# Norm sums and spreads as matrix products, a convolution finish through PSUM, and low weight parts queued behind the taps

## The chip, the cores and the metric

The kernel runs on one core of one Trainium2 chip. The metric is device time in microseconds of one execution. Before the change the median of three runs is 1796.49 us, and they lie between 1795.98 and 1796.54 us.

## What is computed

Two layers over a sequence of 512 tokens with 1024 features, all in float32. Each layer is

```
x = x + 1/2 * SwiGLU_1(RMSNorm(x))                       # 1024 -> 2816 -> 1024
h = RMSNorm(x);  [conv_a | conv_g | q | k | v] = h @ W_in  # five times 512 columns
  conv group: u = a * sigmoid(g); causal depthwise conv, 31 taps; RMSNorm over 512 channels; silu
  diff group: 4 heads, q and k normed per head of 64, two softmax maps with a bias by distance,
              A1 - lambda * A2, times v (128 wide), RMSNorm per head
x = x + concat(conv_out, diff_out) @ W_out
x = x + 1/2 * SwiGLU_2(RMSNorm(x))
```

## The kernel before

**Layout.** Features lie on the 128 partitions and tokens along the free dimension: `x` is eight tiles of 128x512. Every large product is made of three float32r products (`mm3`, L161 to L167): an operand is cut into a high part (rounded to float32r) and a low part (the rest), and high x high, high x low and low x high are summed in PSUM. `parts_of` (L96) makes the parts of a weight chunk: ScalarE copies the high part, and VectorE, or GpSimd where `eng` says so, subtracts to get the low part (L101). `chunk` (L103) loads a chunk through SyncE's DMA queue (SP) and calls it. The rings of weight buffers are five raw, four high and four low.

**The norms.** ScalarE squares each tile of `x`, and GpSimd adds the squares into one tile `s`. `rows_rstd` (L217) transposes the four 128x128 blocks of `s` on TensorE into the PSUM bank "y", VectorE sums each row (L225), scales and adds epsilon (L226), and GpSimd raises to the power -1/2 (L214). This gives a column of 1/rms per token, tokens on partitions. `spread` (L229) brings it back along the free dimension: VectorE multiplies the identity by the column (a diagonal, L241), TensorE multiplies a matrix of ones by that (L245) into bank "y", and ScalarE copies the bank to SBUF (L249). With `split` the column is first cut in two parts, and two float32r products are made. The six norms over 1024 features are in the four feed-forward blocks (split spread) and at the two mixers' inputs (unsplit). The products with the normed input run before the norm is known; its factor is put in when the banks are evicted (L458, L460, L568, L574).

**The feed-forward blocks** use a seven-product scheme on halves (`Halves`, `seven`) for 17 of their 22 column tiles. The change touches only the norm at their start (`first_products` L302, or the lambdas in `ffn` at L450 and L451).

**The mixer** (L541) first makes the convolution's inputs and q, k and v. Then come attention in 16 steps (four query blocks, the last block of tokens first, by four heads) and the convolution's taps:
- A step's scores (`softmaxes`, L714) go into one bank "sc" and one bank "po", two of each. VectorE adds the bias and finds the minimum (L718), ScalarE takes the exp (L722), and VectorE joins the two maps (L725, L727, L728). Two steps later TensorE transposes the map (L735), ScalarE copies it (L737), and a step later TensorE multiplies it by the values (L744).
- After a block's fourth head the per-head norm follows: `se` (L751) and `so` (L755, L756), a power on GpSimd (L214), the multiply `ov` (L759), transposes (L771), and the parts for the out projection (L773, L774).
- `conv_taps`: of the four channel tiles, tile 0 has its 31 taps, and tile 3 ten of its taps, as ScalarE products (L667) summed by GpSimd (L668). VectorE does the others (L680) in bank "y", and joins tile 3's two sums at L684. `conv_square` squares each tile on ScalarE (L654) and adds the squares on GpSimd (L655).
- `conv_finish` (L689) comes after the attention steps in the program's text. It takes the norm of the convolution, then per tile: a GpSimd multiply (L694), a tanh on ScalarE (L696), (tanh + 1) times the value on VectorE (L697), and the high and low parts (L698 on ScalarE, L699 on VectorE).
- The out projection (L815) takes the four convolution tiles first, for all 512 tokens (`ps_out`, 96 products of 512 columns), then the four attention tiles in two halves of the tokens. Its low weight parts are made by GpSimd.

**What sets the order.** The text is not the order. The Tile framework schedules the instructions of each engine by a timeline of its own when the kernel is built, and each engine then runs its queue strictly in that order. `tc.keep_in_program_order` holds single instructions in the text's order. Semaphores and the rings of tiles and banks set the waits.

## Time and profile before

| | us |
|---|---|
| median of 3 runs | 1796.49 |
| the profiled execution | 1796.31 |
| its span on the core | 1794.5 |
| TensorE busy, share of the span | 1784.6 (99%) |
| VectorE busy | 1211.1 (67%) |
| ScalarE busy | 896.1 (50%) |
| GpSimd busy | 653.6 (36%) |

The span is the time between the first and the last instruction of the profiled execution; the execution's own time is 1.8 us longer. PE is TensorE, PEld its weight loads, DVE VectorE, ACT ScalarE, POOL GpSimd and SP SyncE. Products on TensorE overlap, so the duration of one in a group is not what it occupies; the distance between the starts of two is. The granted clock was 1.00 throughout. The names L... in what follows are lines of the kernel before; where a line exists only in the new kernel, the diff shows it.

### The profile page before, as it was taken

What the parts mean: (1) busy time and instruction counts of PE and PEld (TensorE: products, weight loads), DVE (VectorE), ACT (ScalarE), POOL (GpSimd) and SP (SyncE); (2) the same over time, 40 slices, a digit from 0 to 9 for tenths busy, and PEclk for the clock granted to TensorE, in tenths of its full rate; (3) what the DMA queues carried; (4) which work ended last, traced back from release to release, by engine and by line L of the source; (5) the groups of instructions that cost most, each with busy time, mean ns of one, the idle gap of its engine ahead of it and who ended that gap; (6) DMA issues with size and microseconds to landing.
All of it is one profiled execution on the core that took longest, in us unless ns stands there. A gap on an engine that the chain in (4) does not pass through costs nothing.

```text
span 1794.5 us, 28356 instructions
## 1 busy us (share of the span) xinstructions
PE 1784.6 (99%) x10845; PEld 1590.1 (89%) x10845; DVE 1211.1 (67%) x1863; ACT 896.1 (50%) x1482; POOL 653.6 (36%) x460
## 2 busy tenths in 40 slices
PE   9999999999999999999999999999999999999999
PEld 7899899888788899899888998998887888998997
DVE  6976477568867867477576765765788587673762
ACT  6555265445744456256433643654558354552651
POOL 4242232269843132133102312412797331322420
PEclk9999999999999999999999999999999999999999
DMA  7466476323212366466333654663231133664651
GB/s 243 107 179 183 108 181 176 118 94 94 71 48 83 94 165 188 106 171 189 105 94 98 171 167 120 177 179 118 71 114 51 48 106 91 166 178 112 180 150 59
DMA packets 111721, 231.24 MB, mean 129 GB/s; under 512 B 12151, under 2 KB 33414, under 8 KB 111584
## 3 DMA queue, kind: packets, MB, share of 16 engines
q1 hardware_dynamic: 91488, 191.93, 33.4%
q0 software_dynamic: 19808, 37.33, 12.5%
q8 instruction: 85, 1.39, 0.3%
q14 instruction: 52, 0.43, 0.1%
q10 hardware_dynamic: 288, 0.16, 0.0%
HBM read 227.26 MB, written 3.42 MB: 129 GB/s over the span
## 4 chain that ended last, share of the span: by engine, by line
PE 96%; DVE 2%; issue 1%; ACT 1%; DMA 0%; SPq 0%; ACTq 0%; DVEq 0%
PE ps_pair L384 38%; PE ps_d L166 9%; PE ps_d L163 9%; PE ps_d L167 9%; PE ps_pair L167 5%; PE ps_pair L166 5%; PE ps_pair L163 5%; PE ps_pair L596 2%; PE ps_pair L597 2%; PE ps_pair L598 2%; PE ps_out L163 1%; PE ps_out L166 1%; PE ps_sc L714 1%; PE ps_out L167 1%; DVE actl L263 1%; PE ps_v L628 1%
## 5 line engine op out<-in xcount | busy, mean ns | idle before, releaser
L100 ACT ACTIVATE whi<-wraw 128x1024 fp32r<-128x1024 f32 (+2 forms) x599 | 465.9, 802 | 609.5 <-PE ps_pair L384 225.7
L101 DVE TENSOR_TENSOR wlo<-wraw,whi 128x512 fp32r<-128x512 f32 (+2 forms) x556 | 526.0, 968 | 212.6 <-ACT whi L100 208.4
L384 PE MATMUL ps_pair<-acth,wlo 128*128 128x256 f32 x1088 | 308.5, 284 | 0.0
L384 PE MATMUL ps_pair<-actl,whi 128*128 128x256 f32 x1088 | 308.5, 284 | 0.0
L384 PE MATMUL ps_pair<-acth,whi 128*128 128x256 f32 x1088 | 308.4, 283 | 0.0
L166 PE MATMUL ps_d<-hl,whi 128*128 128x512 f32 x704 | 274.2, 390 | 0.0
L167 PE MATMUL ps_d<-hh,wlo 128*128 128x512 f32 x704 | 273.4, 390 | 0.0
L163 PE MATMUL ps_d<-hh,whi 128*128 128x512 f32 x704 | 268.7, 390 | 0.0
L384 PE MATMUL ps_pair<-th,wlo 128*128 128x256 f32 x816 | 231.3, 283 | 0.0
L384 PE MATMUL ps_pair<-tl,whi 128*128 128x256 f32 x816 | 231.2, 283 | 0.0
L384 PE MATMUL ps_pair<-th,whi 128*128 128x256 f32 x816 | 231.2, 283 | 0.0
L146 POOL TENSOR_TENSOR wraw<-wraw 128x512 f32<-128x512 f32 x68 | 101.8, 1497 | 339.5 <-DMA wraw<-in_gu 272.2
L141 POOL DMA_DIRECT2D wraw<-in_gu x68 | 82.0, 1207 | 392.4 <-DMA wraw<-in_gu 228.6
L384 PEld LDWEIGHTS ps_pair<-acth,whi 128*128 128x128 f32 x1088 | 209.1, 192 | 0.3
L384 PEld LDWEIGHTS ps_pair<-actl,whi 128*128 128x128 f32 x1088 | 209.0, 192 | 0.3
L384 PEld LDWEIGHTS ps_pair<-acth,wlo 128*128 128x128 f32 x1088 | 209.1, 192 | 0.0
L480 DVE SCALAR_TENSOR_TENSOR x<-ps_d,x 128x512 f32<-128x512 f32 x96 | 64.7, 689 | 179.6 <-PE ps_d L167 179.3
L166 PE MATMUL ps_pair<-actl,whi 128*128 128x512 f32 x448 | 175.0, 391 | 0.3
L163 PE MATMUL ps_pair<-acth,whi 128*128 128x512 f32 x448 | 174.4, 394 | 0.5 <-ACT whi L100 0.3
L167 PE MATMUL ps_pair<-acth,wlo 128*128 128x512 f32 x448 | 174.5, 391 | 0.0
L384 PEld LDWEIGHTS ps_pair<-tl,whi 128*128 128x128 f32 x816 | 156.7, 192 | 0.7
L384 PEld LDWEIGHTS ps_pair<-th,whi 128*128 128x128 f32 x816 | 156.7, 192 | 0.6
(176 smaller groups left out, 3268.9 us busy)
## 6 DMA issues: line engine op xcount, KB each, us to landing
wraw<-in_gu SPq DMA_DIRECT2D x208, 256.0 KB, 4.0
wraw<-in_gu SPq DMA_DIRECT2D x104, 512.0 KB, 3.7
wraw<-in_gu POOLq DMA_DIRECT2D x68, 512.0 KB, 5.7
wraw<-in_wqkv SPq DMA_DIRECT2D x24, 512.0 KB, 3.7
wraw<-in_dn SPq DMA_DIRECT2D x84, 128.0 KB, 3.1
wraw<-in_dn SPq DMA_DIRECT2D x32, 256.0 KB, 3.1
wraw<-in_wag SPq DMA_DIRECT2D x16, 512.0 KB, 3.6
wraw<-in_wout SPq DMA_DIRECT2D x16, 512.0 KB, 3.6
```

Of the source, the lines that this page charges most:

```text
L100: S.activation(hi, raw, AF.Copy)
L101: (eng or V).tensor_tensor(out=lo, in0=raw, in1=f32(hi), op=ALU.subtract)
L141: nc.gpsimd.dma_start(two.rearrange("p (b c) -> p b c", b=2), u[:, h[0]].unsqueeze(1).broadcast_to([P, 2, 512]), accum_op=ALU.add)
L146: G.tensor_tensor(more[:, h[0]], two[:, h[1]], whole[:, h[0]], op=ALU.add)
L163: first = T.matmul(ps, wh, xh, start=start, stop=False)
L166: T.matmul(ps, wh, xl, start=False, stop=False)
L167: T.matmul(ps, wl, xh, start=False, stop=stop)
L384: mm = T.matmul(ps, l, r, start=first and i == j == 0, stop=False, skip_group_check=True)
L480: V.scalar_tensor_tensor(x[:, m, :], ps, 0.5, x[:, m, :], op0=ALU.mult, op1=ALU.add)
L596: T.matmul(ps[n], xh[:, t], wh, start=k == 0, stop=False)
L597: T.matmul(ps[n], xh[:, t], wl, start=False, stop=False)
L598: T.matmul(ps[n], xl[:, t], wh, start=False, stop=k == KT - 1)
```

## The change

- `rows_rstd` takes a list of sum tiles. For each of the four blocks of 128 tokens it multiplies the block by one column of ones, and sums over the tiles of the list in PSUM. The transposes and the VectorE reduce are gone; the scale by 1/dim and epsilon reads PSUM.
- `spread_bank` replaces the diagonal: four float32 products with the column broadcast over 128 columns as weights and the identity as the moving operand. The split into two parts is gone everywhere.
- The last convolution square is no longer added by GpSimd; it goes into the list as a second tile.
- `conv_finish` stands at attention step 9 in the text, and takes the norm from a call placed right after the taps. VectorE multiplies the value, the gain and the spread, which it reads in its bank; tanh is written to bank "y" and read there by VectorE; the low part is a GpSimd subtraction.
- `se` is a ScalarE square.
- The four weight chunks of the out projection's first half are requested right behind the taps, and their low parts are held in the text's order there (`pin`).

```diff
@@ -93,17 +93,19 @@
         dt = F32 if "raw" in tag else F32R
         return wp.tile([P, n], dt, tag=tag, name=tag, bufs=RING[tag])
-    def parts_of(raw, hi, lo, eng=None, first=False):
+    def parts_of(raw, hi, lo, eng=None, first=False, pin=False):
         if first:
             V.tensor_scalar(hi, raw, 1.0, None, op0=ALU.mult)
         else:
             S.activation(hi, raw, AF.Copy)
-        (eng or V).tensor_tensor(out=lo, in0=raw, in1=f32(hi), op=ALU.subtract)
-    def chunk(src, eng=None):
+        low = (eng or V).tensor_tensor(out=lo, in0=raw, in1=f32(hi), op=ALU.subtract)
+        if pin:
+            tc.keep_in_program_order(low)
+    def chunk(src, eng=None, pin=False):
         raw, hi, lo = ring("wraw"), ring("whi"), ring("wlo")
         nc.sync.dma_start(raw, src)
-        parts_of(raw, hi, lo, eng)
+        parts_of(raw, hi, lo, eng, pin=pin)
         return hi, lo
     def gather(src, blocks, eng=None):
@@ -214,39 +216,33 @@
         G.tensor_tensor(y, v, mhalf[:, :n], op=ALU.pow)
         return y
-    def rows_rstd(s, dim, use="", pin=False):
-        ps = bank("y", "ps_rows")
+    def rows_rstd(sums, dim, use="", pin=False):
+        ps = bank("y", "ps_rows")[:, :NT]
         for j in range(NT):
-            mm = T.transpose(ps[:, j * P : (j + 1) * P], s[:, j * P : (j + 1) * P], ident)
+            for n, s in enumerate(sums):
+                mm = T.matmul(ps[:, j : j + 1], s[:, j * P : (j + 1) * P], ones[:, :1],
+                              start=n == 0, stop=n == len(sums) - 1)
+                if pin:
+                    tc.keep_in_program_order(mm)
+        v = small.tile([P, NT], F32, tag=f"rowv{use}", name="rowv")
+        V.tensor_scalar(v, ps, 1.0 / dim, EPS, op0=ALU.mult, op1=ALU.add)
+        return rsqrt(v, NT, use), v
+    def spread_bank(rc, pin=False):
+        ps = bank("y", "ps_spread")
+        for j in range(NT):
+            mm = T.matmul(ps[:, j * P : (j + 1) * P], rc[:, j : j + 1].broadcast_to([P, P]), ident, start=True, stop=True)
             if pin:
                 tc.keep_in_program_order(mm)
-        v = small.tile([P, NT], F32, tag=f"rowv{use}", name="rowv")
-        V.tensor_reduce(v, ps.rearrange("p (j c) -> p j c", j=NT), axis=AX.X, op=ALU.add)
-        V.tensor_scalar(v, v, 1.0 / dim, EPS, op0=ALU.mult, op1=ALU.add)
-        return rsqrt(v, NT, use), v
-    def spread(rc, tag, pin=False, split=False):
-        parts, dt, left = [rc], F32, ones
-        if split:
-            hi = small.tile([P, NT], F32R, tag="rc_hi", name="rc_hi")
-            V.tensor_scalar(hi, rc, 1.0, None, op0=ALU.mult)
-            lo = small.tile([P, NT], F32, tag="rc_lo", name="rc_lo")
-            V.tensor_tensor(lo, rc, f32(hi), op=ALU.subtract)
-            parts, dt, left = [f32(hi), lo], F32R, ones_r
-        ps = bank("y", "ps_spread")
-        for n, part in enumerate(parts):
-            dg = tmp.tile([P, NT, P], dt, tag=("diag", "sq")[n], name="diag", bufs=1 + n)
-            V.tensor_tensor(
-                dg, ident.unsqueeze(1).broadcast_to([P, NT, P]),
-                part.unsqueeze(2).broadcast_to([P, NT, P]), op=ALU.mult,
-            )
-            mm = T.matmul(ps, left, dg.rearrange("p j c -> p (j c)"), start=n == 0, stop=n == len(parts) - 1)
-            if pin:
-                tc.keep_in_program_order(mm)
+        return ps
+    def spread(rc, tag, pin=False):
         r = act.tile([P, SEQ], F32, tag=tag, name=tag)
-        S.activation(r, ps, AF.Copy)
+        S.activation(r, spread_bank(rc, pin), AF.Copy)
         return r
     class Prep:
@@ -303,11 +299,11 @@
         if not early:
-            rc, v = rows_rstd(pr.s, DM)
-            r = spread(rc, "rb", split=True)
+            rc, v = rows_rstd([pr.s], DM)
+            r = spread(rc, "rb")
         for k in range(KT):
             if early and k == STATS_AT:
-                rc, v = rows_rstd(pr.s, DM, pin=True)
+                rc, v = rows_rstd([pr.s], DM, pin=True)
             for i in range(2):
                 mm3(ps[0][i], wpart(w[0][i], k), pr[k], k == 0, k == KT - 1, pin=early and k in (0, STATS_AT))
         for i in range(2):
@@ -447,8 +443,8 @@
                     if m == 1:
                         _, _, r = first_products(pr, [h[1] for h in held], [h[2] for h in held])
                     elif r is None:
-                        rc = products(pr, w, held[-1][2][0], 0, 4, lambda: rows_rstd(pr.s, DM, pin=True)[0])
-                        r = products(pr, w, held[-1][2][1], 1, 3, lambda: spread(rc, "rb", pin=True, split=True))
+                        rc = products(pr, w, held[-1][2][0], 0, 4, lambda: rows_rstd([pr.s], DM, pin=True)[0])
+                        r = products(pr, w, held[-1][2][1], 1, 3, lambda: spread(rc, "rb", pin=True))
                     else:
                         for i in range(2):
                             products(pr, w, held[-1][2][i], i)
@@ -645,6 +641,7 @@
             ys = [None] * CT
             csum = mp.tile([P, SEQ], F32, tag="csum", name="csum")
+            csums = [csum]
             def conv_square(c, y):
                 if c == 0:
@@ -652,7 +649,10 @@
                 else:
                     sq = mt.tile([P, SEQ], F32, tag="csq", name="csq", bufs=1)
                     S.activation(sq, y, AF.Square)
-                    G.tensor_tensor(csum, csum, sq, op=ALU.add)
+                    if c == CT - 1:
+                        csums.append(sq)
+                    else:
+                        G.tensor_tensor(csum, csum, sq, op=ALU.add)
             def conv_taps(c, n):
@@ -686,17 +686,18 @@
                     S.activation(ys[c], y, AF.Copy)
                 conv_square(c, ys[c])
-            def conv_finish():
-                rcv = spread(rows_rstd(csum, CC, "c")[0], "rb")
+            def conv_finish(rc):
+                rcv = spread_bank(rc)
+                for c in range(CT):
+                    V.scalar_tensor_tensor(ys[c], ys[c], ghalf[l][:, c : c + 1], rcv, op0=ALU.mult, op1=ALU.mult)
                 for c in range(CT):
                     z = ys[c]
-                    hg = ghalf[l][:, c : c + 1]
-                    G.tensor_tensor(z, z, rcv, op=ALU.mult)
-                    th = mt.tile([P, SEQ], F32, tag="gl", name="th", bufs=1)
-                    S.activation(th, z, AF.Tanh, scale=hg)
+                    th = bank("y", "ps_th")
+                    S.activation(th, z, AF.Tanh)
                     V.scalar_tensor_tensor(z, th, 1.0, z, op0=ALU.add, op1=ALU.mult)
-                    S.activation(ch[:, c, :], z, AF.Copy, scale=hg)
-                    V.scalar_tensor_tensor(cl[:, c, :], z, hg, f32(ch[:, c, :]), op0=ALU.mult, op1=ALU.subtract)
+                    S.activation(ch[:, c, :], z, AF.Copy)
+                    G.tensor_tensor(cl[:, c, :], z, f32(ch[:, c, :]), op=ALU.subtract)
             steps = [(i, h) for i in reversed(range(NT)) for h in range(HEADS)]
@@ -748,7 +749,7 @@
                 po = pos[i]
                 se = small.tile([P, HEADS], F32, tag="se", name="se")
-                V.scalar_tensor_tensor(se, sums[i][:, 0, :], VD * EPS, sums[i][:, 0, :], op0=ALU.mult, op1=ALU.mult)
+                S.activation(se, sums[i][:, 0, :], AF.Square, scale=math.sqrt(VD * EPS))
                 sq = tmp.tile([P, SEQ], F32, tag="sq", name="sq")
                 S.activation(sq, po, AF.Square)
                 so = small.tile([P, HEADS], F32, tag="so", name="so")
@@ -806,15 +807,19 @@
                 project_values(NT - 2 - 2 * n)
             for c in range(CT):
                 conv_taps(c, POOL_TAPS[c])
+            rcv = rows_rstd(csums, CC, "c")[0]
+            wo = [chunk(wout[l, 0, n], G, pin=True) for n in range(4)]
             for n in range(2, len(steps) + 5):
                 attend(n)
-            conv_finish()
+                if n == 9:
+                    conv_finish(rcv)
             for half, t in ((0, slice(0, SEQ)), (1, slice(SEQ // 2, SEQ)), (1, slice(0, SEQ // 2))):
                 if t.stop == SEQ:
-                    w = [None] * 4
+                    w = [None] * 4 if half else wo
                 for m in range(KT):
                     if w[m // 2] is None:
                         w[m // 2] = chunk(wout[l, half, m // 2], G)
```

## The prediction

> **What bounds the kernel now.** I read the page first: its engine rows and the chain's shares.

> ```profile
> span 1794.5 us, 28356 instructions
> PE   1784.6 (99%) x10845; PEld 1590.1 (89%) x10845; DVE 1211.1 (67%) x1863; ACT 896.1 (50%) x1482; POOL 653.6 (36%) x460
> PE 96%; DVE 2%; issue 1%; ACT 1%; DMA 0%; SPq 0%; ACTq 0%; DVEq 0%
> ```

> TensorE carries 96% of the chain, so a product added where nothing waits is paid in full, and time saved on another engine counts only where TensorE stands still. The busy figure hides such places, because products overlap; what a product occupies is its pitch, which the merged pieces of the chain give. They come next:

> ```profile
> 481.54 0.45 PE ps_at L735 x4
> 480.01 0.89 PE ps_o L744 x8
> 494.92 0.86 PE ps_spread L245 x2
> 563.97 0.44 PE ps_rows L221 x4
> 564.41 0.23 PE ps_pair L167
> 36.90 0.73 PE ps_spread L245 x2
> ```

> A transpose of 128 columns takes 0.11 us (0.45/4). A full float32 product is two instructions: 128 columns 0.11 us each (0.89/8), 512 columns 0.43 us each, one L245 spread with `ones` 0.86. A float32r product of 512 columns takes 0.23. Today a norm's rows cost 0.44, an unsplit spread 0.86, a split one 2 x 0.23 = 0.46 when its parts are there.

> Then the windows, for the first layer's attention (the second repeats it 891 us later):

> ```profile
> 475.00:490.00 15.00, 14.57 (x84) 10.75 (x83) 12.17 (x45) 13.02 (x36) 12.47 (x10) 1.00 0.38 113
> 490.00:501.70 11.70, 10.19 (x69) 8.23 (x67) 11.49 (x44) 9.05 (x30) 6.29 (x6) 1.00 0.00 0
> 501.70:512.00 10.30, 10.02 (x54) 7.73 (x55) 10.30 (x32) 8.74 (x25) 2.93 (x5) 1.00 0.01 2
> ```

> After the span come TensorE, its weight loads, VectorE, ScalarE, GpSimd. From 490 to 512 VectorE has no free time and ScalarE little: there TensorE waits. Counting the groups of that stretch by pitch: from 475.0 to 501.7, where the first out product starts, 23.6 us of products stand in 26.7; from 475.0 to 529.6, the end of the out projection's first half, 49.7 in 54.6. So 3.1 us are lost before the first out product and 1.8 after it, 4.9 a layer. Nothing else in the run is worth removing from another engine: the waits of TensorE outside attention are under 1.1 us each.

> Last, the timelines of VectorE, GpSimd and the weight loads, for prices:

> ```profile
> 490.54 0.69 DVE L225 TENSOR_REDUCE rowv<-ps_rows 128x4 f32<-128x512 f32 x1
> 493.29 0.69 DVE L241 TENSOR_TENSOR diag<-ident,rs_y 128x512 f32<-128x512 f32 x1
> 499.62 1.29 DVE L697 SCALAR_TENSOR_TENSOR yp<-th,yp 128x512 f32<-128x512 f32 x1
> 502.56 0.68 DVE L697 SCALAR_TENSOR_TENSOR u<-th,u 128x512 f32<-128x512 f32 x1
> ```
> ```profile
> 473.56 4.73 POOL L101 TENSOR_TENSOR wlo<-wraw,whi 128x1024 fp32r<-128x1024 f32 x2
> 489.28 0.20 POOL L756 TENSOR_TENSOR so<-so,se 128x4 f32<-128x4 f32 x1
> 492.16 1.01 POOL L214 TENSOR_TENSOR rs_y<-rowv,mhalf 128x4 f32<-128x4 f32 x1 [1.58 <-DVE rowv L226]
> 498.23 3.64 POOL L694 TENSOR_TENSOR u<-u,rb 128x512 f32<-128x512 f32 x3
> ```
> ```profile
> 5.58 0.19 PEld L166 LDWEIGHTS ps_pair<-actl,whi 128*128 128x128 f32 x1 [0.40 <-DVE actl L263]
> 5.69 0.19 PEld L167 LDWEIGHTS ps_pair<-acth,wlo 128*128 128x128 f32 x1
> 497.86 0.20 PEld L735 LDWEIGHTS ps_at<-ident,e 128*128 128x128 f32 x2 [0.48 <-ACT at L737]
> ```

> **The change, part by part.** *Rows as products with a column of ones.* Each of the six RMSNorms over the model width has four products of one column, eight instructions, for four transposes. No row has a one-column product, but each loads 128x128 weights, and loads outside transposes start no closer than 0.11 us even after an idle spell (5.58 and 5.69). From above I bound one at 0.19 (a load's whole length), from below at 0.06, the distance of the two transpose loads at 497.86 (0.20 less the 0.14 that one lasts). I take 0.11, since these are ordinary float32 loads: 8 x 0.11 = 0.88 for 0.44, +0.44 each, 2.6 us in six (bounds +0.2 and +6.5). Nothing covers it: TensorE is full there.

> *Spreads as broadcast column times identity.* Four float32 products of 128 columns are eight instructions, 0.88. At the four feed-forward norms that replaces a split spread: +0.42 each, 1.7 us. At the two mixers' input norms and the two convolution norms it replaces 0.86: nothing. The VectorE time saved at the six norms (a reduce and one or two diagonals, 0.69 each) falls where TensorE does not wait, and is worth nothing; the shorter way to `r` likewise. If any were late, the next waiters are the evictions at L458 and L568, and their banks.

> *Start-up.* `lamv` no longer shares a buffer with the diagonals, so the built order brings its DMA to the front of GpSimd's queue, and its reduce, exp and `nlam` in among the first conversions of VectorE and ScalarE. The first load, issued at about 1.1, lands near 4.6 (3.5 us by its row), GpSimd multiplies after its scalings at 6.2, and ScalarE's exp ends near 7.2 where L262 began at 6.37 before. Behind it queue L262 and the high parts, which had 0.87 us of waiting for a weight DMA at 8.38: that covers nearly all. The second load sits before the 512-column parts, whose first user on TensorE starts 3.7 us after they are made. I take +0.3, between 0 and 3.

> *The mixer's tail, per layer.* SP's queue is the same row for row, and the weight loads and high parts of `wo` stay where they are; only the low parts move. I walked the built orders from 475.0, where the third step's products start in both, with the durations above.
> - The tenth tap's sum comes 1.27 behind each ScalarE product and, without low parts between them, is ready at 478.1 instead of 485.85. The join L684 then runs at 478.35 ahead of a map update (L728), which it delays by 0.7.
> - The sixteen instructions of the row sums (two tiles; 1.76 instead of 0.44) end at 484.4, the mean (0.16 in place of 0.69 + 0.16) at 484.7, the power at 485.75. GpSimd stands still from 478.1 until then, since the power is next in its queue.
> - Behind the power the four low parts run: 4 x 2.37, to 495.3. Only then come `so` and the power of the first value block (489.28 before), with one `cl` difference between them: 497.8. VectorE reaches the `ov` multiply that needs it at 498.5: covered, by 0.7 us.
> - The spread ends at 488.4. Four scalings by VectorE (0.66 each, the row of L774) run from 488.5 to 491.15. Then each tanh is written to the one bank that the spread used, so tanh, L697, copy, and the next tanh alternate between ScalarE and VectorE, with attention's exps and maps in the same queues. L697 falls at 493.3, 495.3, 498.0 and 501.5.
> - VectorE is relieved of the reduce and diagonal (1.2 in pitch), four `se` (0.3) and the slow form of L697 (0.6), whose 1.29 stood beside a GpSimd multiply. The four scalings replace the four `cl` instructions, but come earlier, inside attention. ScalarE drops `rb` (0.58) and gains four `se` of 0.2. GpSimd's four differences (1.27, as L694) replace four multiplies; one square sum goes.
> - The map update of the twelfth step, whose transposes stand right before the first out product in the built order, ended at 501.9 before. By the walk it ends at 506.4. By VectorE's load alone (+2.6 scalings, +1.3 for three L697 more and the slow one cured, +0.6 for one `ov`, -1.5, +0.4 for idle time) it comes 3.4 later, at 505.3, since in the old order the conversions followed. I take the first out product at 505.5.

> Ahead of it stand 26.3 us of products (23.6 + 1.3 of row sums + 1.4 that stood behind it). The first half's end thus moves by 3.8 (505.5 for 501.7), less 1.4, less 1.2 of the 1.8 lost later, because twelve out products now stand in a row where attention was interleaved with ones and twos: +1.2 us a layer. Bounds: -2.9 if the products alone set the time (first out product at 501.4), +3.2 if each queue is a further 2 us late.

> **Sum.** The profiled execution took 1796.31 us (span 1794.5), 0.2 below the runs' median of 1796.49. 2.6 + 1.7 + 0.3 + 2 x 1.2 = 7.0; 1803.3 us.

> **Rivals.**
> 1. *The tail fills.* If VectorE keeps up, the out products start at 501.4: 2.6 + 1.7 + 0.3 - 5.8 = -1.2, 1795.1, no change; with cheap one-column products as well, 2.4 us less, 1792.7, faster. It decides the sign of the verdict as soon as the first out product starts before 503.8. For it: VectorE has 2.8 us free between 475 and 490 and loses 2.1 us of work. Against: the single bank for tanh, and both queues full from 490 on.
> 2. *One-column products cost next to nothing.* At 0.06 the six norms add 0.2 and the sums in the tail come 0.8 earlier, which passes to the low parts: 0.2 + 1.7 + 0.3 + 2 x 0.4 = 3.0, 1799.3, no measurable change. Against: 0.11 between ordinary loads. [...]
> 3. *Low parts in the way.* If the row sums come more than 0.7 us later than in the walk, `ov` waits on VectorE for GpSimd, and the maps and evictions queued behind it wait too. 2 us a layer more: 1807.3. For it: GpSimd's fixed order; against: the walk's cover.
> 4. *Start-up.* If `lamv` lands as late as the POOL loads of 5.7 us do, twice, ScalarE's first conversions wait: up to 3 us, 1806.

> **How the numbers follow.** About 0.2% (3.6 us) can be told from no change. Forecast 0.50, all slower. Rival 1 0.18: 0.10 no change, 0.08 faster. Rival 2 0.14: 0.10 no change, 0.04 faster. Rival 3 0.12 and rival 4 0.06, slower. Faster 0.12, same 0.20, slower 0.68. The likeliest case alone spans 1800 to 1807. The range takes in rivals 1 to 4 and the dearer one-column load: 1794 to 1810; left out are the cheapest mixture below, and the dear load together with rival 3 above.

> **What would show it.** In the new profile: the pitch of ps_rows and ps_spread pieces (0.88 each); the start of the first L163 into ps_out against 501.73 (505.5); VectorE's `ov` rows with a wait for GpSimd's power (rival 3); ScalarE's wait at the first exp (rival 4); L697 at 0.68 throughout. The forecast is wrong if the first out product comes before 503.8, or if the six norms' products take no longer than before.

## The result and the profile after

The changed kernel took 1808.22 us (median of four runs, 1807.78 to 1808.40), the kernel before 1796.51 beside it: ratio 1.0067, 95% interval [1.0055, 1.0079]. It is slower by 11.7 us, where 7.0 were forecast; 1808.2 lies inside the forecast's range of 1794 to 1810, near its upper end. The profiled execution took 1807.78 us, with a span of 1806.0 against 1794.5.

In what follows L... is a line of the kernel whose profile is shown. In the changed kernel L165, L168 and L169 are the three products of `mm3`, L225 the one-column products, L238 the spread's products, L509 to L515 `lamv`, L693 the scalings, L697 and L698 tanh and (tanh + 1) times the value, L715 the scores, L729 the map update, L736 the transposes, L745 the values.

The page first: the same three rows as before.

```profile
span 1806.0 us, 28501 instructions
PE 1793.3 (99%) x10941; PEld 1601.7 (89%) x10941; DVE 1205.3 (67%) x1827; ACT 894.0 (50%) x1486; POOL 647.2 (36%) x458
PE 95%; DVE 3%; ACT 1%; POOL 1%; issue 1%; DMA 1%; ACTq 0%; DVEq 0%; POOLq 0%
```

VectorE, ScalarE and GpSimd each have less work than before, and TensorE has 96 more instructions. The DMA's share of the chain, 0% before, is now 1%. Next, pieces of the chain at the feed-forward norm behind the first layer's mixer, and at the convolution norm:

```profile
570.35 0.79 PE ps_rows L225 x8
576.97 0.89 PE ps_spread L238 x8
486.26 1.46 PE ps_rows L225 x14
490.88 0.91 PE ps_spread L238 x8
```

A full float32 product is two instructions (the spread's four are the x8 above). Eight one-column instructions take 0.8 to 0.9, as eight of 128 columns do (the third row has fourteen of the sixteen; the other two ran 2.8 us earlier). Then the windows around the first layer's tail (span, TensorE, its loads, VectorE, ScalarE, GpSimd, granted clock, DMA share, GB/s; 478.40 corresponds to 475.0 in the kernel before):

```profile
478.40:493.40 15.00, 15.00 (x95) 11.89 (x94) 12.24 (x37) 11.56 (x32) 7.95 (x5) 1.00 0.07 14
493.40:503.60 10.20, 8.99 (x57) 6.67 (x55) 9.87 (x34) 8.97 (x25) 8.64 (x8) 1.00 0.57 188
503.60:507.00 3.40, 2.09 (x12) 1.26 (x11) 3.36 (x14) 3.40 (x13) 1.86 (x3) 1.00 0.00 0
507.00:510.40 3.40, 3.40 (x18) 3.32 (x17) 2.29 (x10) 1.48 (x7) 1.18 (x2) 0.50 0.00 0
```

From 493.4 to 507 VectorE is busy for 13.23 and ScalarE for 12.37 of 13.60 us, TensorE for 11.08. Then comes a thing that the trace of before has nowhere ahead of its last products: 3.4 us in which the granted clock is 0.50, called half clock below.

**Where the time went.** Pairing every TensorE product of the new trace with the same product of the old one gives the shift of each, and where the shift grows. The last product comes 11.47 us later:

| stretch | forecast | measured |
|---|---|---|
| start-up with the first feed-forward norm (to 60 us) | 0.3 + 0.86 | 2.89 |
| mixer input norms, first and second layer | 0.44, 0.44 | 0.52, 0.56 |
| mixer tail, first layer | 1.2 | 2.95 |
| mixer tail, second layer | 1.2 | 1.86 |
| the three other feed-forward norms | 3 x 0.86 | 0.91, 0.90, 0.88 |
| sum | 7.0 | 11.47 |

The start is the noisiest term: in the three experiments whose start-up is that of the kernel before, the shift at 60 us is -0.59, -0.31 and -0.22.

The start-up's chain in the changed kernel, from the second load of `lamv` to the product that waits:

```profile
9.58 6.03 DMA lamv<-in_lamv
15.69 0.60 POOL lamv L511 x2
16.32 0.30 DVE lamd L513
16.70 0.20 ACT lame L515
16.90 1.56 ACT whi L100 x3
18.46 1.84 ACT acth L258 x3
20.31 0.52 ACT ssum L267
...
26.20 1.31 POOL ssum L271
...
28.07 1.05 ACT whi L100
29.14 2.17 DVE wlo L101
31.36 0.50 PE ps_pair L169
```

Both layers' `lamv` share one buffer, so the second load stands in GpSimd's queue behind the first layer's products of it (6.15 to 6.88) and the scalings queued after them. It is issued at 9.58 and is there at 15.6. ScalarE stands in front of the exp for 3.27 us. Everything behind it in its queue (high parts, squares, and through the squares GpSimd's sum) comes later: the first square starts at 20.21 instead of 17.92. TensorE waits 1.5 us at 31.36 for that low part.

### The profile page after: what moved, and what is told of

The parts are those of the page before. It is cut to its first block, busy times and chain, and to the rows that moved or that the text cites. A ratio compares the mean times of both kernels' runs of the same rounds, so it can differ in the third digit from the quotient of the medians.

```text
span 1806.0 us, 28501 instructions
## 1 busy us (share of the span) xinstructions
PE 1793.3 (99%) x10941; PEld 1601.7 (89%) x10941; DVE 1205.3 (67%) x1827; ACT 894.0 (50%) x1486; POOL 647.2 (36%) x458
## 4 chain that ended last, share of the span: by engine, by line
PE 95%; DVE 3%; ACT 1%; POOL 1%; issue 1%; DMA 1%; ACTq 0%; DVEq 0%; POOLq 0%
PE ps_pair L380 38%; PE ps_d L165 9%; PE ps_d L168 9%; PE ps_d L169 9%; PE ps_pair L169 5%; PE ps_pair L168 5%; PE ps_pair L165 5%; PE ps_sc L715 2%; PE ps_pair L593 2%; PE ps_pair L594 2%; PE ps_pair L592 2%; PE ps_out L169 1%; PE ps_out L165 1%; PE ps_out L168 1%; DVE actl L259 1%; PE ps_v L624 1%
## 5 line engine op out<-in xcount | busy, mean ns | idle before, releaser
L101 DVE TENSOR_TENSOR wlo<-wraw,whi 128x512 fp32r<-128x512 f32 (+2 forms) x556 | 529.4, 974 | 229.2 <-ACT whi L100 215.8
L168 PE MATMUL ps_d<-hl,whi 128*128 128x512 f32 x704 | 273.9, 389 | 0.0
L169 PE MATMUL ps_d<-hh,wlo 128*128 128x512 f32 x704 | 273.2, 389 | 0.0
L165 PE MATMUL ps_d<-hh,whi 128*128 128x512 f32 x704 | 269.3, 389 | 0.0
L169 PE MATMUL ps_pair<-acth,wlo 128*128 128x512 f32 x448 | 174.5, 391 | 1.5 <-DVE wlo L101 1.5
L165 PE MATMUL ps_pair<-acth,whi 128*128 128x512 f32 x448 | 174.1, 392 | 1.1 <-ACT whi L100 1.1
L168 PE MATMUL ps_pair<-actl,whi 128*128 128x512 f32 x448 | 174.8, 391 | 0.3
```

The costliest lines, as they stand in the source:

```text
L101: low = (eng or V).tensor_tensor(out=lo, in0=raw, in1=f32(hi), op=ALU.subtract)
L165: first = T.matmul(ps, wh, xh, start=start, stop=False)
L168: T.matmul(ps, wh, xl, start=False, stop=False)
L169: T.matmul(ps, wl, xh, start=False, stop=stop)
```

## The experiments

Each kernel ran beside the kernel before on the same chip, which took 1796.0 there. The medians are compared by their distance to it; the changed kernel stands at +11.7. The shifts at each stretch come from each run's profile; an asterisk marks a stretch with half clock in it. Executions of one kernel can differ by more than the terms compared (the five of rows_old lie between 1803.24 and 1805.84), so terms below 1 us are read from the profiles' shifts and not from the medians.

| kernel | median | over before | start | mixer inputs | ff norms | tail 1 | tail 2 |
|---|---|---|---|---|---|---|---|
| changed kernel | 1808.2 | +11.7 | 2.89 | 0.52, 0.56 | 0.91, 0.90, 0.88 | 2.95* | 1.86 |
| lam_two | 1805.0 | +9.1 | 0.57 | 0.52, 0.55 | 0.85, 0.91, 0.82 | 2.93* | 1.85 |
| rows_old | 1805.3 | +9.3 | 4.46* | 0.06, 0.07 | 0.41, 0.44, 0.38 | 1.82 | 1.85 |
| split_lam | 1803.3 | +7.4 | 0.16 | 0.43, 0.46 | 0.41, 0.47, 0.40 | 1.84 | 3.02* |
| tail_old | 1804.5 | +8.5 | 3.06 | 0.51, 0.51 | 0.85, 0.91, 0.82 | -0.23 | -0.15 |
| one_tile | 1803.3 | +7.3 | 1.15 | 0.52, 0.55 | 0.89, 0.91, 0.87 | 1.14 | 1.22 |
| th_sbuf | 1814.6 | +18.6 | 1.15 | 0.52, 0.55 | 1.56, 0.91, 0.88 | 6.47* | 6.99* |
| low_free | 1803.4 | +7.5 | 0.50 | 0.52, 0.56 | 0.89, 0.91, 0.86 | 1.36* | 1.52* |
| one_scale | 1801.9 | +5.9 | 0.25 | 0.52, 0.56 | 1.52, 0.90, 1.49 | 0.04 | 0.08 |
| mended | 1803.1 | +7.1 | 0.24 | 0.51, 0.56 | 0.88, 0.91, 0.88 | 0.56 | 0.64 |
| tail_new | 1798.8 | +2.8 | -0.59 | 0, 0 | 0, 0, 0 | 1.29 | 1.32* |
| spread4 | 1795.8 | -0.3 | -0.31 | 0, 0 | 0, 0, 0 | -0.12 | -0.10 |
| hold_only | 1799.1 | +3.1 | -0.22 | 0, 0 | 0, 0, 0 | 1.52 | 1.58 |

**lam_two: the start-up.**

```diff
-            t = tmp.tile([P, SEQ], F32, tag="diag", name="lamv", bufs=1)
+            t = tmp.tile([P, 6 * HD], F32, tag="diag", name="lamv", bufs=2)
```

> The kernel after, with two buffers for lamv instead of one, so that the second layer's load no longer waits for the first layer's products of it. Theory: the start-up's 2.0 us (shift of 2.9 at 80 us less 0.86 for the norm there) come from VectorE's 2.7 us and ScalarE's 3.3 us of waiting for that load at 16 us; with both loads issued by 3 us they land before 7, the waits go, and the time is 1808.2 - 2.0 = 1806.2. Rival: the start-up is later because the reordered queues themselves cost it (exp and reduce among the conversions, squares behind them); then at most 0.5 comes back, 1807.7 or more.

Measured 1805.04 (ratio 1.0049 [1.0037, 1.0062]). The shift at 60 us falls from 2.89 to 0.57. In the five other kernels with two buffers it is 0.24 to 1.15. ScalarE's timeline shows the queue without the wait:

```profile
9.28 0.19 ACT L515 ACTIVATE lame<-lamd 128x2 f32<-128x2 f32 x1
11.63 0.19 ACT L515 ACTIVATE lame<-lamd 128x2 f32<-128x2 f32 x1
17.76 0.62 ACT L267 ACTIVATE ssum<-x 128x512 f32<-128x512 f32 x1
```

The same two exps stand among the conversions, and the squares start at 17.76, as early as before. So the reordering itself costs next to nothing, and the one load that waits for a buffer costs 2.3 us, give or take the 0.9 by which the kernels with two buffers differ. The kernel tail_old, with one buffer, has 3.06.

**rows_old: the six norms' rows by transposes again.**

```diff
     def rows_rstd(sums, dim, use="", pin=False):
+        if len(sums) == 1:
+            ps = bank("y", "ps_rows")
+            for j in range(NT):
+                mm = T.transpose(ps[:, j * P : (j + 1) * P], sums[0][:, j * P : (j + 1) * P], ident)
...
+            V.tensor_reduce(v, ps.rearrange("p (j c) -> p j c", j=NT), axis=AX.X, op=ALU.add)
```

> The kernel after, with the rows of the six norms over 1024 features as before (four transposes and a VectorE reduce); the convolution norm's rows stay one-column products. Theory: eight instructions at 0.11 us against four, 0.44 us less at each of six norms, 2.6 us: 1805.6. Rival: the one-column products are no dearer than transposes where TensorE has other work queued: 1808.2, no change. Second rival: the reduce (0.69) and its place in VectorE's queue delay the first evictions behind each norm and cost back half: 1806.9.

Measured 1805.25 (1.0048 [1.0035, 1.0061]). Away from the start, five norms lose 0.46, 0.49, 0.50, 0.46 and 0.50 of their shift: the forecast's +0.44 each, and neither rival. That the median comes out 2.4 nearer to the kernel before, close to the 2.6 forecast, is chance: in the profile the half clock is gone from the first tail (-1.1) and stands in the start-up (4.46, where 2.89 less a norm's 0.44 would leave 2.45).

```profile
29.17:32.58 3.41, 1.48 (x5) 0.96 (x6) 2.96 (x2) 3.41 (x5) 3.25 (x3) 1.00 0.00 0
32.58:36.00 3.42, 3.42 (x10) 2.56 (x10) 3.42 (x3) 0.38 (x1) 0.87 (x2) 0.50 0.72 222
```

These two windows of rows_old are TensorE waiting for the late conversions, and the 3.41 us behind them at half clock.

**split_lam: the six norms' spreads by diagonals again**, split at the feed-forward norms, with `lamv` back on the diagonals' buffer.

```diff
-    def spread(rc, tag, pin=False):
+    def spread(rc, tag, pin=False, split=False):
...
-            r = spread(rc, "rb")
+            r = spread(rc, "rb", split=True)
```

> The kernel after, with the spreads of the six norms over 1024 features as before (diagonals and products with ones, split in two float32r parts in the feed-forward blocks); the diagonals share their buffer with lamv again, so lamv's loads come late as before. The convolution norm's spread stays four products. Theory: 4 x 0.42 = 1.7 for the spreads and 2.0 for the start-up: 1804.5. Rival: the spread is covered, and only the start-up comes back: 1806.2. If the start-up is not due to lamv, 1806.5.

Measured 1803.33 (1.0038 [1.0024, 1.0052]). The three later feed-forward norms cost 0.41, 0.47 and 0.40 instead of 0.91, 0.90 and 0.88, so a spread of four products is dearer than a split one by 0.43 to 0.50; 0.42 was forecast. The start falls to 0.16, by 2.7 where 2.0 was forecast; that is 0.7 of the 1.2 us by which the median lies below the theory's 1804.5. Here the half clock stands in the second layer's tail and the first layer's costs 1.84: the same work, and the stretch has moved.

**tail_old: the mixer's tail as before.** The diff shows the order of the calls only; the old finish, the rows by transposes of one sum tile and the old `se` come with it, and the spread is four products copied to SBUF.

```diff
...
-            rcv = rows_rstd(csums, CC, "c")[0]
-            wo = [chunk(wout[l, 0, n], G, pin=True) for n in range(4)]
             for n in range(2, len(steps) + 5):
                 attend(n)
-                if n == 9:
-                    conv_finish(rcv)
+            conv_finish()
+            wo = [None] * 4
```

> The kernel after, with the mixer's tail as before: the convolution's finish at the end of the text with the GpSimd multiply, its norm's rows by transposes of one sum tile, se on VectorE, the out projection's low weights unheld. The six norms over 1024 features and lamv's place stay as in the kernel after; the convolution's spread is four products copied to SBUF. Theory: the tail cost 1.86 us in the second layer and 2.95 in the first, of which 1.1 is a stretch at half clock from 507.0 to 510.3 us that follows TensorE's stalls; both go: 1808.2 - 4.8 = 1803.4, granted clock 1.00 throughout. Rival: the half clock has nothing to do with the tail's stalls and stays: 1804.5. Rival: the out projection starts as late for another reason: over 1806.

Measured 1804.46 (1.0045 [1.0032, 1.0057]). In the profiled execution (1802.69, no half clock) both tails cost nothing, -0.23 and -0.15. The four other executions list a mean clock of 0.999 and are 1.3 to 2.0 us longer; where in them the clock fell is not recorded, and the median lies where the first rival put it. So the tail's cost goes with the tail. Half clock is not the tail's alone: rows_old shows it in the start-up.

The next four start from lam_two (1805.0), to take the tail apart.

**one_tile: one sum tile for the convolution norm.**

```diff
-                    if c == CT - 1:
-                        csums.append(sq)
-                    else:
-                        G.tensor_tensor(csum, csum, sq, op=ALU.add)
+                    G.tensor_tensor(csum, csum, sq, op=ALU.add)
```

> The kernel with two lamv buffers (1805.0 us), with the last convolution square added by GpSimd as before, so that the convolution's row sums are eight instructions instead of sixteen. Theory, products set the tail: 0.88 us less on TensorE in each layer, 1805.0 - 1.8 = 1803.3. Rival, VectorE's queue sets the first out product: the saved products only lengthen the waits before it, 1805.0. Second rival: the added sum (1.27 us on GpSimd) delays the rows, and with them the low parts and the value norm's power behind them; 1806 or more, with VectorE's ov multiply waiting for GpSimd.

Measured 1803.26 (1.0041 [1.0028, 1.0053]). The tails fall from 1.85 (where there was no half clock) to 1.14 and 1.22, by 0.6 to 0.7 of the 0.88 removed: less than products alone would give, far more than the first rival. That the median meets the theory's 1803.3 is in part luck: the half clock is gone too (no execution of this kernel shows a reduced clock), and the start is 0.6 later. GpSimd's extra sum ran while it stood idle.

**low_free: the out projection's low weights unheld.**

```diff
-            wo = [chunk(wout[l, 0, n], G, pin=True) for n in range(4)]
...
-                    w = [None] * 4 if half else wo
+                    w = [None] * 4
```

> The kernel with two lamv buffers (1805.0 us), with the out projection's first four chunks made where they were in the text before and their low parts unheld: the built order puts them between the tap sums of the convolution's last tile again. Theory: the tap sum is ready some 7 us later (485 against 478 in the frame of the kernel before), the norm, the scalings and the tanh slip with it into the part where VectorE is full, and the tail grows by 2 us a layer: 1809. Rival: VectorE's load decides and the order of the finish does not matter; 1805, within 0.7.

Measured 1803.44 (1.0039 [1.0025, 1.0053]): neither. GpSimd makes the low parts between tap sums again, the norm's power comes at 491.3 instead of 485.7, and yet the tails are shorter, 1.36 and 1.52, with half clock in both. The early norm that the holding buys is worth less than nothing. The theory that a later finish lengthens the tail is wrong here.

**one_scale: three of four scalings left out.**

```diff
-                for c in range(CT):
+                for c in range(1):
                     V.scalar_tensor_tensor(ys[c], ys[c], ghalf[l][:, c : c + 1], rcv, op0=ALU.mult, op1=ALU.mult)
```

> The kernel with two lamv buffers (1805.0 us), with three of the four scalings of the convolution's tiles by VectorE left out (their values go to tanh without norm and gain): 1.98 us less on VectorE in each layer, every product still there. The built order of the tail shifts a little with it. Theory, VectorE's load sets the first out product: the tail is 1.5 to 2 us shorter in each layer, 1801.5. Rival, the products set it: 1805.0, within 0.5. If in between, both bind in turn.

Measured 1801.89 (1.0033 [1.0020, 1.0045]). The tails fall to 0.04 and 0.08: 1.8 us for 1.98 us of VectorE's time. VectorE's load sets the tail, as the theory says. The feed-forward norm behind it gives 0.6 back (1.52 and 1.49); why was not followed.

**th_sbuf: tanh in SBUF.**

```diff
-                    th = bank("y", "ps_th")
+                    th = mt.tile([P, SEQ], F32, tag="prod", name="th")
```

> The kernel with two lamv buffers (1805.0 us), with tanh written to two SBUF buffers (the ring of the taps' products, free by then) instead of the one PSUM bank. Theory, VectorE is full there: (tanh + 1) times the value has both operands in SBUF again and takes up to 1.29 us beside GpSimd instead of 0.69, up to 4 x 0.6 more a layer; some 1.2 of it reaches the first out product, 1807.4. Rival, the single bank is what delays the finish: tanh no longer waits for it and the first out product comes up to 1 us earlier, 1803.

Measured 1814.60 (1.0103 [1.0090, 1.0117]), far beyond both. These are the four products of (tanh + 1) and the value in VectorE's timeline, and GpSimd's low parts beside them:

```profile
493.11 1.69 DVE L698 SCALAR_TENSOR_TENSOR yp<-th,yp 128x512 f32<-128x512 f32 x1
495.19 2.36 DVE L698 SCALAR_TENSOR_TENSOR u<-th,u 128x512 f32<-128x512 f32 x1
498.60 0.68 DVE L698 SCALAR_TENSOR_TENSOR u<-th,u 128x512 f32<-128x512 f32 x1
499.79 1.14 DVE L698 SCALAR_TENSOR_TENSOR u<-th,u 128x512 f32<-128x512 f32 x1
```
```profile
487.23 9.77 POOL L101 TENSOR_TENSOR wlo<-wraw,whi 128x1024 fp32r<-128x1024 f32 x4
```

With both operands in SBUF the same instruction takes up to 2.36 beside GpSimd's row, about one low part (9.77/4 = 2.44). At 498.60 it takes 0.68; there GpSimd's four-column sum `so`, which started 0.05 later, is the longer one: 0.69 instead of 0.20. With tanh in PSUM all of them take 0.68 or 0.69. The 3.1 us of stretching come where VectorE is full, and with TensorE's gaps there (7.12 us busy of the 11.70 from 490.0) come 6.83 and 10.24 us of half clock in the two tails; how the rest of the loss divides between the two was not measured.

**mended: three prices together** (two `lamv` buffers, one sum tile, low parts unheld: the diffs of lam_two, one_tile and low_free).

> The kernel after with three of its parts taken back together: two lamv buffers, the last convolution square added by GpSimd, the out projection's low parts unheld. The six norms' products, the four-product spreads and the finish at step 9 stay. Theory, the three prices add: 1805.0 (two buffers) less 1.8 (one sum tile) less 1.6 (unheld) = 1801.6. Rival, VectorE sets the tail in all of them and the saved products do not count twice: 1803.

Measured 1803.10 (1.0040 [1.0027, 1.0053]). The median is the rival's number. The profiled execution, without half clock, took 1801.54, the theory's, with tails of 0.56 and 0.64: against one_tile, which has no half clock either, the unheld low parts save another 0.58 a layer, so there the savings do count together. The other four list clocks of 0.997 to 0.999 and took 1802.97 to 1804.59. That half clock is what parts them from the profiled one fits these clocks, but no trace of them was kept. And the theory's 1.6 for the low parts came from two runs with half clock in their tails, so its exact sum is luck.

The last three start from the kernel before.

**tail_new: the new finish alone.**

```diff
-            conv_finish()
+                if n == 9:
+                    conv_finish(rcv)
```

(with the new `conv_finish`, its `spread_bank`, and `se` on ScalarE; the rows by transposes of one sum tile, ahead of the loop)

> The kernel before (1796.0) with only the new finish: four-product spread read in its bank, the four scalings on VectorE, tanh in the bank, low parts of the result on GpSimd, se on ScalarE, the finish at step 9 of the text. The norm's rows stay transposes of one sum tile, the low weights unheld, lamv and the six norms as before. Theory: with unheld low parts the tail lost 0.4 us a layer without a half-clock stretch, one sum tile gives back 0.7 and transposes 0.44, so 0.7 less a layer than before: 1794.5. Rival: the finish inside attention takes VectorE's time from the maps and costs its 1 us a layer whatever the rows do: 1798; a half-clock stretch in a run adds 1.1.

Measured 1798.81 (1.0017 [1.0008, 1.0025]). The theory fell: 1.29 and 1.32 a layer, although its products are those of the kernel before to within 0.02 us. The rival fits: the finish costs VectorE's time. TensorE's worst window in the second layer, ahead of a stretch at half clock, has VectorE without a gap:

```profile
1389.30:1392.73 3.43, 0.87 (x4) 0.66 (x5) 3.43 (x13) 2.32 (x7) 1.36 (x3) 1.00 0.00 0
```

One comparison on record says more. The tails of mended have the same finish, one sum tile and unheld low parts; they differ in the rows, which are one-column products there and transposes with a VectorE reduce (0.69) here. With half as many products for the rows, these tails are 0.7 longer (1.29 and 1.32 against 0.56 and 0.64). So with the new finish, where VectorE is full, the one-column rows go with the shorter tail. The built orders differ as well, so it is not shown that the reduce alone makes the 0.7.

**hold_only: the held low weights alone.**

```diff
+            wo = [chunk(wout[l, 0, n], G, pin=True) for n in range(4)]
             for n in range(2, len(steps) + 5):
...
-                    w = [None] * 4
+                    w = [None] * 4 if half else wo
```

> The kernel before (1796.0) with only the out projection's low weights moved: the first four chunks made right behind the taps in the text and their low parts held there. Theory: the held parts stand on GpSimd before the value norms' power and the finish, which costs 0.8 us a layer, as between the kernels with held and unheld parts: 1797.6. Rival: with the old finish they free the tap sums (7 us earlier) and fill a stretch in which GpSimd waits: 1794.5.

Measured 1799.10 (1.0016 [1.0008, 1.0025]): 1.5 us a layer, twice the theory, and the opposite of the rival. VectorE's timeline has three instructions that are longer than elsewhere, two of them beside GpSimd's row of low parts (482.05 to 491.29), the third beside its multiplies (497.87 to 502.3):

```profile
485.02 1.73 DVE L228 TENSOR_SCALAR rowv<-rowv 128x4 f32<-128x4 f32 x1
487.49 1.56 DVE L753 SCALAR_TENSOR_TENSOR se<-sums 128x4 f32<-128x4 f32 x1
501.48 1.37 DVE L699 SCALAR_TENSOR_TENSOR yp<-th,yp 128x512 f32<-128x512 f32 x1
```

The first two work on four columns; L228 takes 0.17 elsewhere, `se` 0.16, and the product of (tanh + 1) and the value 0.68. All read only SBUF. Right behind the first two TensorE waits 1.38 us, at 489.92, for VectorE's minimum, a wait that the kernel before does not have. That the stretching is all of the 1.5 us was not tested by itself.

**spread4: the four-product spread alone, copied to SBUF.**

```diff
-                rcv = spread(rows_rstd(csum, CC, "c")[0], "rb")
+                rcv = act.tile([P, SEQ], F32, tag="rb", name="rb")
+                S.activation(rcv, spread_bank(rows_rstd(csum, CC, "c")[0]), AF.Copy)
```

> The kernel before (1796.0) with only the convolution norm's spread as four products with the identity, copied to SBUF as before: one VectorE diagonal (0.69) less in each layer, TensorE 0.88 instead of 0.86. Theory: VectorE is full there, so the tail is 0.2 us shorter in each layer, as it was with the old tail in the changed kernel (shifts of -0.23 and -0.15): 1795.6. Rival: no change, 1796.0.

Measured 1795.75 against 1796.03 (0.9998 [0.9989, 1.0007]): not to be told from no change. The tails' -0.12 and -0.10 are half of the forecast. Of the three parts put alone into the kernel before it is the only one that does no harm, and no version that ran beats that kernel by more than can be measured.

## Why the prediction was right, and where it was short

**Rows.** Right. The one-column instructions start 0.110 to 0.113 us apart (60 of 70 distances in the changed kernel), against the 0.11 taken from ordinary loads, and a norm's rows cost 0.46 to 0.50 more, against 0.44. Rival 2, with its 0.06, is out: the other ten distances, 26 to 30 ns, stand only between the first two instructions of a group, whose first load was made beside an earlier product. Each instruction has its own load in the trace, and from the second of a group on the loads start 0.108 to 0.113 us apart as well.

**Spreads.** Right: 0.43 to 0.50 against 0.42, and next to nothing at the mixers' inputs beyond their rows (0.52 and 0.56 there, of which 0.06 and 0.07 stay with old rows).

**Start-up.** The step that failed most: the term of +0.3, measured 2.3 by lam_two (2.89 - 0.57). The forecast covered the second load with the 3.7 us until the first user of the 512-column parts. But the wait stands in ScalarE's and VectorE's queues, and what is queued behind the parts has no such cover: squares, GpSimd's seven sums one after another, then the conversion of 1024 columns. It was rival 4's mechanism, with one load of 6.03 us instead of two late ones, and it had been given 0.06.

**The tail.** The walk held to within 1 us, the term of +1.2 did not. Taking 899.6 from the second layer's times (its shift of 8.73 at that point, and 890.87 between the layers of the kernel before):

| | walk | measured |
|---|---|---|
| join of the tenth tap's sum (L684) | 478.35 | 478.43 |
| end of the power | 485.75 | 485.6 |
| scalings | 488.5 to 491.15 | 488.4 to 491.1 |
| end of the low parts | 495.3 | 494.9 |
| L698, four starts | 493.3, 495.3, 498.0, 501.5 | 493.0, 495.05, 497.0, 500.7 |
| map update before the first out product, end | 506.4; 505.3 by load | 505.5 |
| first out product | 505.5 | 506.5 |

These are the measured rows of VectorE, GpSimd and TensorE, and the load of the first out product in the kernel before, 501.73 (the multiply `ov`, L760, follows without a wait, so rival 3 did not happen, nor did rival 1):

```profile
1392.63 0.68 DVE L698 SCALAR_TENSOR_TENSOR yp<-ps_th,yp 128x512 f32<-128x512 f32 x1
1394.65 0.68 DVE L698 SCALAR_TENSOR_TENSOR u<-ps_th,u 128x512 f32<-128x512 f32 x1
1396.62 0.69 DVE L698 SCALAR_TENSOR_TENSOR u<-ps_th,u 128x512 f32<-128x512 f32 x1
1397.22 0.68 DVE L760 TENSOR_TENSOR ov<-ps_o,rs_y 128x512 f32<-128x512 f32 x1
1400.32 0.69 DVE L698 SCALAR_TENSOR_TENSOR u<-ps_th,u 128x512 f32<-128x512 f32 x1
...
1404.66 0.48 DVE L729 SCALAR_TENSOR_TENSOR e<-ps_sc,c,e 128x256 f32<-128x256 f32 x1
```
```profile
1385.17 9.33 POOL L101 TENSOR_TENSOR wlo<-wraw,whi 128x1024 fp32r<-128x1024 f32 x4
1395.83 1.02 POOL L216 TENSOR_TENSOR rs_y<-so,mhalf 128x4 f32<-128x4 f32 x1
```
```profile
1405.16 0.71 PE L745 MATMUL ps_o<-vv,at 128*128 128x128 f32 x4
...
1405.93 0.38 PE L736 MATMUL ps_at<-ident,e 128*128 128x128 f32 x2
1406.07 0.48 PE L165 MATMUL ps_out<-acth,whi 128*128 128x512 f32 x1
```
```profile
501.73 0.19 PEld L163 LDWEIGHTS ps_out<-acth,whi 128*128 128x128 f32 x1 [1.50 <-ACT acth L698]
```

The map came on time, at 1405.14, but TensorE then still had four instructions of value products (L745, 1405.16) and two of scores in its queue ahead of that map's transposes (1405.93), which the forecast had not put there. So the first out product is 1.0 later and the tail costs 1.86, not 1.2. That VectorE's load and the row sums both set it is shown: 1.98 us off VectorE gives 1.8, 0.88 us off TensorE gives 0.6 to 0.7.

**What was not in the forecast at all:** 1.1 us of half clock in the first layer's tail (2.95 against 1.86 for the same instructions). Start-up (2.0 short), tails (0.66 each) and half clock (1.1) make 4.4 of the 4.5 us by which the shift exceeds the forecast; the first norm came out 0.3 cheaper, which is within what the start-up varies by, and the other five together 0.3 dearer. So the norms' 4.3 us and the sign were right for the reasons given. That the time fell inside the range was in part luck: a term that the forecast did not have used up room that had been left for rivals 3 and 4.

## What to carry to other kernels

A wait that moves to the front of an in-order queue is covered only as far as everything queued behind it is covered; follow the queue to the first product that lacks something, not to the first user of the next row. Where one engine is full, the sum of its durations forecasts the delay well (1.98 us off VectorE gave 1.8), and every term that is added to it must pay. And on TensorE the instructions of a one-column product started 0.110 to 0.113 us apart, with their weight loads at 0.108 to 0.113, and a product has two of them; a transpose of 128 columns took 0.11 in all, so a one-column product did not beat it there. It can pay only where the engine that it relieves is the full one.

## What the runs showed of the hardware

- **Half clock after gaps.** In the changed kernel TensorE's granted clock falls to 0.50 at 507.0 for 3.41 us, and a pair of products that occupies 0.27 in the second layer occupies 0.43 in the first (from the start of the pair to that of the next row):

```profile
507.03 0.64 PE L715 MATMUL ps_sc<-kt,qz 128*128 128x128 f32 x2
507.46 1.06 PE L745 MATMUL ps_o<-vv,at 128*128 128x128 f32 x4
...
1403.20 0.39 PE L715 MATMUL ps_sc<-kt,qz 128*128 128x128 f32 x2
1403.47 0.71 PE L745 MATMUL ps_o<-vv,at 128*128 128x128 f32 x4
```
